# Attention of a decoder trunk: scores, softmax and transposes of two heads together, products with the values by fours

## The chip, the core and the metric

The kernel runs on one core of one Trainium2 chip. The metric is the time of one execution on the device, in microseconds (us). Three runs of the kernel before gave 1165.54, 1167.07 and 1168.0 us; the median is 1167.07.

## What is computed

A trunk of two layers over 256 tokens of width 1024, in float32. Each layer is a half-step SwiGLU feed-forward, a mixer, and another half-step feed-forward, each behind an adaptive RMS norm. The mixer of layer 0 is a gated MLP, that of layer 1 is the attention that the change is about. It has 16 heads of 64, one key block of 256 keys, so that each query sees the causal part of its own block, with a bias by head and distance:

```
q, k, v = split(h @ w_qkv)                    # 16 heads of 64
logits  = q @ k.T / 8 + rel_bias[bucket(distance)]
logits  = where(distance >= 0, logits, -1e30)
o       = softmax(logits) @ v
x       = x + gate * (o @ w_o)
```

## The kernel before

All activations lie on chip; the weights stream from memory. Tokens are two tiles of 128 (t = 0, 1). A product (`gemm`) goes over K tiles of 128: `split_weights` loads two K tiles at a time, ScalarE takes the first part of each weight (a cast) and VectorE the second (a subtraction), and TensorE multiplies in three terms (high with both weight parts, low with the first), each instruction 128 x 512. `gemm` is a generator: it yields after each K tile, and `interleave(steps, calls)` puts other work behind a given step in program order. `tick` hangs one piece of background work (the modulation vectors of later sublayers: a load, and two VectorE steps at L114) behind certain K tiles. The program is then scheduled ahead of time: instructions stand in each engine's queue by the order of the program, by when their inputs were expected, and by when buffers come free, so an engine's queue is not the program's order word for word. At run time each queue is worked in order.

The attention is `moba`, from L642. Its stages:

- The product "qk0" gives q and k of heads 0 to 7, "qk1" those of heads 8 to 15, "vv" gives v. `leave_qk` copies q and k out of the accumulators (L654 on VectorE, L656 on ScalarE) into `half_tile` buffers, of which there are four in all. `turn_qk` transposes them (L386) into qT and kT, in which two heads lie one above the other: an even head in partitions 0 to 63, the odd one in 64 to 127.
- `scores(hd)` does one head. For each of the two query blocks: a product of 64 rows, 128 x 128 or 128 x 256 (L676), a reduction on VectorE that adds the bias and gives the negated maximum (L678), the exponential with its sum on ScalarE (L681). Both query blocks lie in the same accumulator bank. Then the reciprocal (L683) and the scaling (L686). Its `lg` is a `half_tile`.
- `turn(hd)` transposes the head's three 128 x 128 blocks of probabilities (L693) and ScalarE copies them out (L702).
- `mix(hd)` multiplies by the values (L712, L713): the output of an even head goes to partitions 0 to 63, that of an odd head to 64 to 127. Behind each fourth head ScalarE copies the bank to oT (L715).
- `project` multiplies oT by w_o, adds the residual and starts the next norm.

There are six accumulator banks ("acc"), of which a product holds four, and two banks for transposes ("tr"). Weights in two parts, the bias of eight heads, and v share eight buffers ("hl"). Step n of qk1 carries the scores of one head and the transposes of the head two before, and so does each step of vv, some with two. The first fifteen heads' transposes thus run beside products; the products with the values come after vv, in the first two steps of `project` too. The second half of the bias is loaded behind step 5 of qk1.

Of the kernel before, what the change touches and what calls it, by code (L numbers as in the profile page):

```python
# [40 lines left out]
def bucket_onehot():  # L41
    """Column i stands for the distance i - 127; the columns of negative distances are zero."""
    m = np.zeros((NBUCK, EW), np.float32)
    for n in range(S):
        if n < MAX_EXACT:
            b = n
        else:
            b = MAX_EXACT + int(
                math.log(n / MAX_EXACT) / math.log(MAX_DIST / MAX_EXACT) * (NBUCK - MAX_EXACT)
            )  # L50
        m[min(b, NBUCK - 1), P - 1 + n] = 1.0
    return m
# [3 lines left out]
def trunk(ctx: ExitStack, tc: tile.TileContext, x, c, rel_bias, mod_w, mod_b, norm_g,  # L56
# [18 lines left out]
    def small(name, w=1):  # L75
        return stat.tile([P, w], F32, tag=f"st{w}", name=name)
# [16 lines left out]

# [1 line left out]
    def mod_unit(i, s, part):  # L95
        """Steps that end with vector `part` of sublayer (i, s) over all partitions."""
        col = (s * 3 + part) * D
# [51 lines left out]

# [1 line left out]
    raws = {}  # L151
    ready = {}

    def split_weights(src, key, kt, cols):
        """K tile kt of the columns in cols, [P, 2 parts, columns]; a load carries two K tiles."""
        if (key, kt) in ready:
            return ready.pop((key, kt))
        w = sum(cw for _, cw in cols)
        if kt % 2 == 0:
            if w > 512:  # L160
                r = pool.tile([P, 2, D], F32, tag="raw", name=f"raw_{key}_{kt}", bufs=3)
            else:
                r = pool.tile([P, 2, 512], F32, tag="ahl", name=f"raw_{key}_{kt}", bufs=4)
            n = min(2, src.shape[0] // P - kt)
            runs, o = [], 0
            for c0, cw in cols:
                if runs and runs[-1][0] + runs[-1][1] == c0:
                    runs[-1][1] += cw
                else:
                    runs.append([c0, cw, o])  # L170
                o += cw
            for c0, cw, o in runs:
                nc.sync.dma_start(
                    r[:, :n, o:o + cw],
                    src[kt * P:(kt + n) * P, c0:c0 + cw].rearrange("(k p) n -> p k n", p=P))
            raws[key] = r
        r = raws[key]
        hl = hl_slot([P, 2, D], F32R, f"hl_{key}_{kt}")
        nc.scalar.copy(hl[:, 0, :w], r[:, kt % 2, :w])  # L179
        nc.vector.tensor_sub(hl[:, 1, :w], r[:, kt % 2, :w], hl[:, 0, :w].bitcast(F32))  # L180
        return hl
# [5 lines left out]
    def gemm(src, key, cols, lhs, ps, lead_first=0, lead_last=0, early=0, after_first=None, ticks=4):  # L187
        """Fills ps with accumulators [P tokens, columns] by (token tile, column range)."""
        nk = src.shape[0] // P
# [68 lines left out]
    def row_rstd(t, name):  # L258
        """(mean of squares + eps) ** -0.5 of a row of x"""
        ss = []  # L260
# [15 lines left out]
    def to_columns(src, hi, lo, name):  # L276
        """[P tokens, 4 * P] -> two exact parts of its transpose."""
        ps = tr_bank(f"tr_{name}")
# [55 lines left out]
    def act_lhs(a):  # L334
        """Two exact parts of stored activations, by pairs of K tiles."""
        pairs = {}
# [20 lines left out]
    def project(i, s, src, a, lead=LEAD, early=0):  # L357
        """Steps of the product that ends a sublayer, its residual and the next adaLN."""
        ps = {}
# [12 lines left out]
    def interleave(steps, calls):  # L372
        """calls[n] come after step n."""
        for n, _ in enumerate(steps):
            for f, *a in calls.get(n, ()):
                f(*a)
# [4 lines left out]
    def store_act(a, src, w, k0, t, name):  # L381
        """[P tokens, w] -> a[:, k0.., tokens of t]"""
        n = w // P
# [8 lines left out]

# [1 line left out]
    def ffn_gate(g, n, w):  # L394
# [32 lines left out]
    def head(w_in):  # L427
        """The first adaLN by blocks of columns, its products running as the blocks come."""
        src = mod_w[0].rearrange("(p k) n -> p k n", k=KD)
# [105 lines left out]

# [1 line left out]
    def gmlp(i, s):  # L537
# [78 lines left out]

# [1 line left out]
    bias = {}  # L618

    def bias_table():  # L620
        """Scaled bias by head and distance, in DRAM; what the mask hides is at the start."""
        oh = half_tile("oh")[:NBUCK, :EW]
# [12 lines left out]
    def load_bias(b):  # L635
        """[query, head, distances that go down with the key]"""
        bias[b] = hl_slot([P, HEADS // 2, S], F32, f"bias{b}")
# [4 lines left out]
    def moba(i, s):  # L642
# [7 lines left out]
        def leave_qk(n, t, ps):  # L650
            for h in range(2):
                rows[n, t, h] = half_tile(f"q{n}{t}{h}")
                if h == 0:
# [11 lines left out]

        def scores(hd):
            j, po = hd // 2, (hd % 2) * HD
            ps = acc_bank(f"sc{hd}")
            lg = half_tile(f"lg{hd}")
            nm, z, rz = (small(f"{a}{hd}", 2) for a in ("nm", "z", "rz"))  # L670
            b = bias[hd // 8][:, hd % 8, :]
            for qb in range(NT):
                n = P * (qb + 1)
                sl = slice(off[qb], off[qb] + n)
                one = slice(qb, qb + 1)
                nc.tensor.matmul(ps[:, sl], qT[po:po + HD, j, qb * P:(qb + 1) * P],  # L676
                                 kT[po:po + HD, j, :n], start=True, stop=True)
                nc.vector.tensor_tensor_reduce(  # L678
                    lg[:, sl], ps[:, sl], b[:, n - 1::-1], scale=-(HD ** -0.5), scalar=-NEG,
                    op0=ALU.add, op1=ALU.min, accum_out=nm[:, one])  # L680
                nc.scalar.activation(lg[:, sl], lg[:, sl], AF.Exp, bias=nm[:, one], scale=-1.0,  # L681
                                     accum_out=z[:, one])
            nc.vector.reciprocal(rz, z)  # L683
            for qb in range(NT):
                sl = slice(off[qb], off[qb] + P * (qb + 1))
                nc.vector.tensor_scalar_mul(lg[:, sl], lg[:, sl], rz[:, qb:qb + 1])  # L686
            probs[hd] = lg

        def turn(hd):
            pr = probs.pop(hd)  # L690
            tp = tr_bank(f"tp{hd}")
# [12 lines left out]

        def mix(hd):
            j, po = hd // 2, (hd % 2) * HD
            if hd % 4 == 0:
                ovs[0] = acc_bank(f"ov{hd}")
            o = ovs[0][po:po + HD, (j % 2) * S:(j % 2) * S + S]
            pT, vs = pTs.pop(hd), held["v"]  # L710
            cols = slice(hd * HD, (hd + 1) * HD)
            nc.tensor.matmul(o, vs[:, 0, cols], pT[:, 0:S], start=True, stop=False)  # L712
            nc.tensor.matmul(o[:, P:], vs[:, 1, cols], pT[:, S:S + P], start=False, stop=True)  # L713
            if hd % 4 == 3:
                nc.scalar.copy(oT[:, j - 1:j + 1, :], ovs[0].rearrange("p (j n) -> p j n", j=2))  # L715

# [6 lines left out]
                        ticks=2, after_first=lambda: leave_qk(1, 0, qk2)), {  # L723
            0: [(turn_qk, 0, 0), (turn_qk, 0, 1), (scores, 0)], 1: [(scores, 1)],
            2: [(scores, 2), (turn, 0)], 3: [(scores, 3), (turn, 1)],
            4: [(scores, 4), (turn, 2)], 5: [(scores, 5), (turn, 3), (load_bias, 1)],
            6: [(scores, 6), (turn, 4)]})
        leave_qk(1, 1, qk2)
        vp = {}

        def leave_v(t):
            if t == 0:
# [5 lines left out]
                        after_first=lambda: leave_v(0)), {  # L738
            0: [(scores, 7), (turn, 5), (turn_qk, 1, 0), (turn_qk, 1, 1)],
            1: [(scores, 8), (turn, 6), (scores, 9)], 2: [(scores, 10), (turn, 7)],  # L740
            3: [(scores, 11), (turn, 8)], 4: [(scores, 12), (turn, 9)],
            5: [(scores, 13), (turn, 10), (scores, 14), (turn, 11)],
            6: [(scores, 15), (turn, 12)]})
        leave_v(1)
        turn(13)
        for hd in range(5):
            mix(hd)
        turn(14)
        for hd in range(5, 8):
            mix(hd)  # L750
        turn(15)
        interleave(project(i, s, w_o, oT, early=4),
                   {0: [(mix, 8), (mix, 9), (mix, 10), (mix, 11)],
                    1: [(mix, 12), (mix, 13), (mix, 14), (mix, 15)]})

# [1 line left out]
    new_hT()  # L757
# [43 lines left out]
```

## Time and profile before

| | before |
|---|---|
| runs (three), us | 1165.54, 1167.07, 1168.0 |
| median, us | 1167.07 |
| the profiled execution, span from the first to the last instruction, us | 1163.7 |
| the profiled execution, time of its own | not given beside the span |
| TensorE busy | 1139.9 us, 98% |
| TensorE weight loads | 946.8 us, 81% |
| VectorE busy | 828.7 us, 71% |
| ScalarE busy | 592.8 us, 51% |
| GpSimd busy | 32.2 us, 3% |
| mean DMA rate | 241 GB/s |

Times in the profile count from the start of the span. TensorE's matmuls are pipelined: their records overlap, so the time between the starts of two neighbours tells more than the length of one. A float32 matmul stands as two records. "idle before" an instruction is the time its engine stood still, with what released it.

### The profile page before, as it was taken

The page shows a single profiled execution, that of the slowest core. Times are in us where ns is not written, and L with a number is a line of the kernel's source. Part 1 is how long each engine was busy: PE and PEld are TensorE (multiplying, and loading weights), DVE is VectorE, ACT ScalarE, POOL GpSimd, SP SyncE. Part 2 cuts the span into 40 slices and gives each one's busy share as a digit, 9 for nine tenths or more (in the row PEclk, how much of TensorE's full clock was granted, in tenths as well). Part 3 has the DMA queues.
Part 4 walks back from the last instruction along what each step waited for, and adds up shares of the span by engine and source line. Part 5 has one row for each costly group of instructions (what it writes and reads, how often), then busy time and mean ns, then how long its engine had stood idle before and what let it go on. Part 6 is the DMA issues. An engine that isn't in the chain of part 4 may idle for free.

```text
span 1163.7 us, 14007 instructions
## 1 busy us (share of the span) xinstructions
PE 1139.9 (98%) x5381; PEld 946.8 (81%) x5381; DVE 828.7 (71%) x1008; ACT 592.8 (51%) x849; POOL 32.2 (3%) x42
## 2 busy tenths in 40 slices
PE   6999999999999999999999999999999999999997
PEld 4788998878878887888988788998777678889985
DVE  3887787935797888584778776678888668554553
ACT  3465454446555544563553545555366466554541
POOL 0000000000000000000000000000000000000000
PEclk9999999999999999999999999999999999999999
DMA  9787888548688585784978657687696355555640
GB/s 336 274 347 266 302 317 305 198 152 276 225 329 325 215 327 201 269 286 139 316 254 325 219 195 260 205 299 281 229 331 222 131 181 169 176 176 166 217 145 37
DMA packets 86538, 279.99 MB, mean 241 GB/s; under 512 B 4980, under 2 KB 15284, under 8 KB 86472
## 3 DMA queue, kind: packets, MB, share of 16 engines
q1 hardware_dynamic: 86472, 279.10, 68.4%
q8 instruction: 42, 0.69, 0.2%
q14 instruction: 24, 0.20, 0.0%
HBM read 278.01 MB, written 1.07 MB: 240 GB/s over the span
## 4 chain that ended last, share of the span: by engine, by line
PE 90%; DVE 5%; DMA 2%; issue 1%; POOL 1%; ACT 1%; SPq 0%; POOLq 0%; DVEq 0%
PE ps_o L201 24%; PE ps_g L201 19%; PE ps_u L201 19%; PE ps_gu L201 6%; PE ps_v L201 5%; PE ps_qk L201 3%; PE ps_vv L201 2%; PE ta L386 2%; DMA mw<-in_mod_w_dram 2%; PE sc L676 1%; PE mps L132 1%; DVE hl_g L180 1%; PE hps L465 1%; PE sv L609 1%; PE ps_u00a L201 1%
## 5 line engine op out<-in xcount | busy, mean ns | idle before, releaser
L201 PE MATMUL ps_o<-hl_o,ahl 128*128 128x512 f32 x1440 | 334.4, 391 | 0.9 <-ACT ahl L342 0.9
L201 PEld LDWEIGHTS ps_o<-hl_o,ahl 128*128 128x128 f32 x1440 | 269.0, 188 | 56.2 <-ACT ahl L342 1.1
L201 PE MATMUL ps_g<-hl_g,hTh 128*128 128x512 f32 (+1 forms) x768 | 203.7, 376 | 0.7 <-ACT hTh L498 0.7
L179 ACT CAST hl_o<-raw_o 128x1024 fp32r<-128x1024 f32 x120 | 125.9, 1053 | 112.7 <-PE ps_o L201 72.4
L180 DVE TENSOR_TENSOR hl_o<-raw_o,hl_o 128x1024 fp32r<-128x1024 f32 x120 | 145.9, 1222 | 50.2 <-ACT hl_o L179 49.5
L201 PE MATMUL ps_u<-hl_u,hTh 128*128 128x512 f32 (+1 forms) x704 | 181.5, 369 | 0.0
L114 DVE SCALAR_TENSOR_TENSOR ma<-mw,cs,ma 128x1024 f32<-128x1024 f32 x128 | 163.9, 1280 | 15.9 <-DMA mw<-in_mod_w_dram 15.4
L201 PEld LDWEIGHTS ps_g<-hl_g,hTh 128*128 128x128 f32 x768 | 141.6, 189 | 21.7 <-ACT hTh L498 1.4
L180 DVE TENSOR_TENSOR hl_g<-raw_g,hl_g 128x1024 fp32r<-128x1024 f32 (+1 forms) x96 | 107.6, 1132 | 56.7 <-ACT hl_g L179 56.3
L201 PEld LDWEIGHTS ps_u<-hl_u,hTh 128*128 128x128 f32 x704 | 129.7, 188 | 17.6
L179 ACT CAST hl_g<-raw_g 128x1024 fp32r<-128x1024 f32 (+1 forms) x96 | 91.9, 980 | 101.7 <-PE ps_u L201 88.2
L180 DVE TENSOR_TENSOR hl_u<-raw_u,hl_u 128x1024 fp32r<-128x1024 f32 (+1 forms) x88 | 98.5, 1127 | 61.5 <-ACT hl_u L179 60.8
L201 PE MATMUL ps_g<-hl_g,hTl 128*128 128x512 f32 (+1 forms) x384 | 121.3, 376 | 0.0
L179 ACT CAST hl_u<-raw_u 128x1024 fp32r<-128x1024 f32 (+1 forms) x88 | 85.5, 974 | 61.5 <-PE ps_g L201 56.2
L201 PE MATMUL ps_u<-hl_u,hTl 128*128 128x512 f32 (+1 forms) x352 | 108.6, 369 | 0.0
L201 PEld LDWEIGHTS ps_g<-hl_g,hTl 128*128 128x128 f32 x384 | 71.3, 189 | 11.1 <-issue 1.3
L201 PEld LDWEIGHTS ps_u<-hl_u,hTl 128*128 128x128 f32 x352 | 65.4, 188 | 8.7
L201 PE MATMUL ps_gu<-hl_gu,hTh 128*128 128x512 f32 x192 | 55.0, 394 | 0.0
L201 PE MATMUL ps_v<-hl_v,hTh 128*128 128x512 f32 x192 | 54.2, 392 | 0.3 <-ACT hl_v L179 0.3
L180 DVE TENSOR_TENSOR hl_v<-raw_v,hl_v 128x1024 fp32r<-128x1024 f32 x24 | 28.8, 1221 | 27.4 <-ACT hl_v L179 25.0
L201 PEld LDWEIGHTS ps_v<-hl_v,hTh 128*128 128x128 f32 x192 | 35.8, 188 | 8.2 <-ACT hl_v L179 0.5
L201 PEld LDWEIGHTS ps_gu<-hl_gu,hTh 128*128 128x128 f32 x192 | 35.8, 188 | 7.1
(160 smaller groups left out, 1226.3 us busy)
## 6 DMA issues: line engine op xcount, KB each, us to landing
mw<-in_mod_w_dram SPq DMA_DIRECT2D x64, 1024.0 KB
raw_o<-in_ffn_w_out_dram SPq DMA_DIRECT2D x44, 1024.0 KB
raw_g<-in_ffn_w_in_dram SPq DMA_DIRECT2D x32, 1024.0 KB
raw_u<-in_ffn_w_in_dram SPq DMA_DIRECT2D x28, 1024.0 KB
raw_g<-in_ffn_w_in_dram SPq DMA_DIRECT2D x16, 768.0 KB
raw_u<-in_ffn_w_in_dram SPq DMA_DIRECT2D x16, 768.0 KB
raw_v<-in_gmlp_w_in_dram SPq DMA_DIRECT2D x12, 1024.0 KB
raw_gu<-in_gmlp_w_in_dram SPq DMA_DIRECT2D x12, 1024.0 KB
```

Source lines behind the costliest of these rows:

```text
L114: nc.vector.scalar_tensor_tensor(st["acc"], w[:, j, :], cs[:, k0 + j:k0 + j + 1], st["acc"], op0=ALU.mult, op1=ALU.add)
L132: nc.tensor.matmul(ps, lhs, hl[:, j, sl], start=j == 0, stop=j == 1)
L179: nc.scalar.copy(hl[:, 0, :w], r[:, kt % 2, :w])
L180: nc.vector.tensor_sub(hl[:, 1, :w], r[:, kt % 2, :w], hl[:, 0, :w].bitcast(F32))
L201: nc.tensor.matmul(ps[t, h][:, :cw], lhs(k, t)[p], hls[k][:, wp, o:o + cw], start=k == 0 and p == 0 and wp == 0, stop=k == nk - 1 and p == 1)
L386: nc.tensor.transpose(ps[:, j * P:(j + 1) * P], src[:, j * P:(j + 1) * P], ident)
L465: nc.tensor.matmul(ps[part], cb[:, k, :], w[:, k, :], start=False, stop=k == KD - 1)
L609: nc.tensor.matmul(sv[:, sl], wsT[:, g, :], v[n][:, t, lo - n * D:hi - n * D], start=True, stop=True)
L676: nc.tensor.matmul(ps[:, sl], qT[po:po + HD, j, qb * P:(qb + 1) * P], kT[po:po + HD, j, :n], start=True, stop=True)
```

## The change

`scores` takes a pair of heads: all four products of the pair come first, alternating between the two heads, each head in a bank of its own; the reductions and exponentials of both heads follow. The reciprocal and the scaling become a function of their own, `norm`, one step later. `turns` transposes both heads of a pair, two steps behind its scores. `mix` takes four heads at a time. The rows of q and k go to the buffers "sg" (four, used by the gates of the feed-forward and by the last transposed probabilities) and no longer to the four `half_tile` buffers. The second half of the bias is loaded behind step 3 of qk1, before behind step 5. The diff also drops comments and docstrings all through the file, which moves line numbers.

```diff
-                rows[n, t, h] = half_tile(f"q{n}{t}{h}")
+                rows[n, t, h] = pool.tile([P, 512], F32, tag="sg", name=f"q{n}{t}{h}", bufs=4)
...
-        def scores(hd):
-            j, po = hd // 2, (hd % 2) * HD
-            ps = acc_bank(f"sc{hd}")
...
-                nc.tensor.matmul(ps[:, sl], qT[po:po + HD, j, qb * P:(qb + 1) * P],
-                                 kT[po:po + HD, j, :n], start=True, stop=True)
...
+        def scores(pair):
+
+            hds = (2 * pair, 2 * pair + 1)
+            ps, lg = {}, {}
+            for hd in hds:
+                ps[hd] = acc_bank(f"sc{hd}")
             for qb in range(NT):
                 n = P * (qb + 1)
                 sl = slice(off[qb], off[qb] + n)
...
+                for hd in hds:
+                    po = (hd % 2) * HD
+                    nc.tensor.matmul(ps[hd][:, sl], qT[po:po + HD, pair, qb * P:(qb + 1) * P],
+                                     kT[po:po + HD, pair, :n], start=True, stop=True)
...
+            for hd in hds:
+                lg = half_tile(f"lg{hd}")
+                nm, z, rz = (small(f"{a}{hd}", 2) for a in ("nm", "z", "rz"))
+                b = bias[hd // 8][:, hd % 8, :]
+                for qb in range(NT):
...
+                    nc.vector.tensor_tensor_reduce(
+                        lg[:, sl], ps[hd][:, sl], b[:, n - 1::-1], scale=-(HD ** -0.5),
+                        scalar=-NEG, op0=ALU.add, op1=ALU.min, accum_out=nm[:, one])
+                    nc.scalar.activation(lg[:, sl], lg[:, sl], AF.Exp, bias=nm[:, one],
+                                         scale=-1.0, accum_out=z[:, one])
+                probs[hd] = (lg, z, rz)
+
+        def norm(pair):
+            for hd in (2 * pair, 2 * pair + 1):
+                lg, z, rz = probs[hd]
+                nc.vector.reciprocal(rz, z)
+                for qb in range(NT):
+                    sl = slice(off[qb], off[qb] + P * (qb + 1))
+                    nc.vector.tensor_scalar_mul(lg[:, sl], lg[:, sl], rz[:, qb:qb + 1])
...
+        def turns(pair):
+            turn(2 * pair)
+            turn(2 * pair + 1)
+
+        def mix(four):
+
+            ov = acc_bank(f"ov{four}")
+            vs = held["v"]
+            for pair in (2 * four, 2 * four + 1):
+                for hd in (2 * pair, 2 * pair + 1):
...
-            0: [(turn_qk, 0, 0), (turn_qk, 0, 1), (scores, 0)], 1: [(scores, 1)],
-            2: [(scores, 2), (turn, 0)], 3: [(scores, 3), (turn, 1)],
-            4: [(scores, 4), (turn, 2)], 5: [(scores, 5), (turn, 3), (load_bias, 1)],
-            6: [(scores, 6), (turn, 4)]})
+            0: [(turn_qk, 0, 0), (turn_qk, 0, 1), (scores, 0)], 1: [(norm, 0)],
+            2: [(turns, 0), (scores, 1)], 3: [(norm, 1), (load_bias, 1)],
+            4: [(turns, 1), (scores, 2)], 5: [(norm, 2)],
+            6: [(turns, 2), (scores, 3)]})
...
-            0: [(scores, 7), (turn, 5), (turn_qk, 1, 0), (turn_qk, 1, 1)],
-            1: [(scores, 8), (turn, 6), (scores, 9)], 2: [(scores, 10), (turn, 7)],
-            3: [(scores, 11), (turn, 8)], 4: [(scores, 12), (turn, 9)],
-            5: [(scores, 13), (turn, 10), (scores, 14), (turn, 11)],
-            6: [(scores, 15), (turn, 12)]})
+            0: [(norm, 3), (turn_qk, 1, 0), (turn_qk, 1, 1)], 1: [(turns, 3), (scores, 4)],
+            2: [(norm, 4)], 3: [(turns, 4), (scores, 5)], 4: [(norm, 5)],
+            5: [(turns, 5), (scores, 6)], 6: [(norm, 6), (scores, 7)]})
         leave_v(1)
-        turn(13)
-        for hd in range(5):
-            mix(hd)
-        turn(14)
-        for hd in range(5, 8):
-            mix(hd)
-        turn(15)
-        interleave(project(i, s, w_o, oT, early=4),
-                   {0: [(mix, 8), (mix, 9), (mix, 10), (mix, 11)],
-                    1: [(mix, 12), (mix, 13), (mix, 14), (mix, 15)]})
+        mix(0)
+        turns(6)
+        mix(1)
+        norm(7)
+        mix(2)
+        interleave(project(i, s, w_o, oT, early=4), {0: [(turns, 7)], 1: [(mix, 3)]})
```

## Rows read from the trace of the kernel before

**Rows 1.** The page: the span, and the shares of the chain that ended last.

```profile
span 1163.7 us, 14007 instructions
PE 90%; DVE 5%; DMA 2%; issue 1%; POOL 1%; ACT 1%; SPq 0%; POOLq 0%; DVEq 0%
```

**Rows 2.** Busy time by stretch: the columns stand in the first line.

```profile
core 0: us, PE busy (x) PEld busy (x) DVE busy (x) ACT busy (x) POOL busy (x), PEclk, DMA share, GB/s
844.00:862.00 18.00, 17.99 (x82) 14.75 (x81) 17.00 (x17) 11.15 (x14) 0.96 (x1) 1.00 0.89 319
...
862.00:934.00 72.00, 71.98 (x315) 48.46 (x313) 51.12 (x134) 42.38 (x101) 0.00 (x0) 1.00 0.56 195
...
934.00:951.00 17.00, 16.07 (x108) 11.52 (x108) 12.51 (x21) 12.66 (x23) 0.00 (x0) 1.00 0.74 241
```

**Rows 3.** The chain in order of time: start, length, what; an undisturbed product.

```profile
1037.70 21.77 PE ps_u L201 x96
```

**Rows 4.** TensorE's timeline, one turn: start, length, line, operation, shape, count.

```profile
877.54 0.49 PE L676 MATMUL sc<-actm 64*128 64x128 f32 x2
877.96 0.55 PE L693 MATMUL tp<-ident,lg 128*128 128x128 f32 x3
878.26 1.17 PE L201 MATMUL ps_qk<-hl_qk,hTh 128*128 128x512 f32 x4
879.27 0.39 PE L201 MATMUL ps_qk<-hl_qk,hTl 128*128 128x512 f32 x1
879.59 0.70 PE L676 MATMUL sc<-actm 64*128 64x256 f32 x2
880.21 0.50 PE L201 MATMUL ps_qk<-hl_qk,hTl 128*128 128x512 f32 x1
880.55 1.09 PE L201 MATMUL ps_qk<-hl_qk,hTh 128*128 128x512 f32 x4
881.48 0.62 PE L201 MATMUL ps_qk<-hl_qk,hTl 128*128 128x512 f32 x2
882.02 0.49 PE L676 MATMUL sc<-actm 64*128 64x128 f32 x2
```

**Rows 5.** Weight loads of scores: by shape (busy, mean ns), then one on the timeline.

```profile
L676 PEld LDWEIGHTS sc<-actm 64*128 64x128 f32 x64 | 9.4, 184 | 10.6 <-issue 6.6 <-DVE lg L686 2.4 <-DVE vs L735 0.4
...
882.02 0.29 PEld L676 LDWEIGHTS sc<-actm 64*128 64x128 f32 x2 [0.36 <-issue]
```

**Rows 6.** TensorE's timeline, products with the values and the gap between them.

```profile
935.20 0.65 PE L712 MATMUL ov<-pT,vs 128*64 128x256 f32 x2
...
936.40 0.32 PE L713 MATMUL ov<-pT,vs 128*64 128x128 f32 x1
936.41 0.43 PE L712 MATMUL ov<-pT,vs 128*64 128x256 f32 x1
...
941.25 0.50 PE L201 MATMUL ps_o<-hl_o,ahl 128*128 128x512 f32 x1 [0.93 <-ACT ahl L342]
...
944.40 0.66 PE L712 MATMUL ov<-actm,vs 128*64 128x256 f32 x4
...
945.91 3.02 PE L201 MATMUL ps_o<-hl_o,ahl 128*128 128x512 f32 x12
```

**Rows 7.** Busy time from 862 to 934 us: tile lg, then L678, L683, L686, L180, L114.

```profile
862.00:934.00 72.00, 6.51 (x36) 3.79 (x36) 17.51 (x58) 16.43 (x60) 1.00 0.56 195
...
862.00:934.00 72.00, 10.86 (x60) 1.00 0.56 195
...
862.00:934.00 72.00, 2.41 (x15) 1.00 0.56 195
...
862.00:934.00 72.00, 7.65 (x28) 1.00 0.56 195
...
862.00:934.00 72.00, 14.39 (x13) 1.00 0.56 195
...
862.00:934.00 72.00, 15.35 (x12) 1.00 0.56 195
```

**Rows 8.** SP's queue: the issue of the bias load of heads 8 to 15.

```profile
861.77 0.37 SPq L639 DMA_DIRECT2D bias<-ed  x1
```

More of the change, by code (lines that the diff above doesn't have):

```diff
@@ L664, in moba @@
         held = {}
-        def scores(hd):
-            j, po = hd // 2, (hd % 2) * HD
-            ps = acc_bank(f"sc{hd}")
-            lg = half_tile(f"lg{hd}")
-            nm, z, rz = (small(f"{a}{hd}", 2) for a in ("nm", "z", "rz"))
-            b = bias[hd // 8][:, hd % 8, :]
+        def scores(pair):
[3 more added lines that the diff above has]
+                ps[hd] = acc_bank(f"sc{hd}")
             for qb in range(NT):
@@ L674, in scores @@
                 sl = slice(off[qb], off[qb] + n)
-                one = slice(qb, qb + 1)
-                nc.tensor.matmul(ps[:, sl], qT[po:po + HD, j, qb * P:(qb + 1) * P],
-                                 kT[po:po + HD, j, :n], start=True, stop=True)
[L678 to L687, printed above, removed]
+                for hd in hds:
+                    po = (hd % 2) * HD
+                    nc.tensor.matmul(ps[hd][:, sl], qT[po:po + HD, pair, qb * P:(qb + 1) * P],
+                                     kT[po:po + HD, pair, :n], start=True, stop=True)
@@ new lines, in scores @@
+            for hd in hds:
[3 more added lines that the diff above has]
+                for qb in range(NT):
+                    n = P * (qb + 1)
+                    sl = slice(off[qb], off[qb] + n)
+                    one = slice(qb, qb + 1)
+                    nc.vector.tensor_tensor_reduce(
[4 more added lines that the diff above has]
+                probs[hd] = (lg, z, rz)
@@ L689, in turn @@
+        def norm(pair):
[5 more added lines that the diff above has]
+                    nc.vector.tensor_scalar_mul(lg[:, sl], lg[:, sl], rz[:, qb:qb + 1])
         def turn(hd):
-            pr = probs.pop(hd)
+            pr = probs.pop(hd)[0]
             tp = tr_bank(f"tp{hd}")
@@ L703, in turn @@
             pTs[hd] = pT
[L705 to L715, printed above, removed]
+        def turns(pair):
[6 more added lines that the diff above has]
+                for hd in (2 * pair, 2 * pair + 1):
+                    po = (hd % 2) * HD
+                    o = ov[po:po + HD, (pair % 2) * S:(pair % 2) * S + S]
+                    pT = pTs.pop(hd)
+                    cols = slice(hd * HD, (hd + 1) * HD)
+                    nc.tensor.matmul(o, vs[:, 0, cols], pT[:, 0:S], start=True, stop=False)
+                    nc.tensor.matmul(o[:, P:], vs[:, 1, cols], pT[:, S:S + P], start=False,
+                                     stop=True)
+            nc.scalar.copy(oT[:, 2 * four:2 * four + 2, :], ov.rearrange("p (j n) -> p j n", j=2))
         qk = {}
```

## The prediction

> **What bounds the kernel now.** I read the chain of work that ended last first. It belongs to TensorE for 90% of the span [rows 1], so a change of the attention stage pays only by what it takes off TensorE's own line there. Then the busy time of each engine by stretch: over the two products that the scores run beside (862 to 934 us) TensorE is busy for 71.98 of 72.00 us, VectorE for 51.12 (71%), ScalarE for 42.38, at a granted clock of 1.00 (the level of 2.4 GHz) in every stretch [rows 2]. Nobody keeps TensorE waiting; what it spends beyond the plain products is the price of the small matmuls between them. The chain gives the price of a plain product, 21.77 us for 96, so 0.227 us [rows 3].
>
> Then TensorE's timeline for one turn of the present pattern, one head's two scores, another head's three transposes and twelve plain products [rows 4]. From one 64x128 score to the next are 4.48 us. Twelve products are 2.72; the transposes take 0.30 (877.96 to 878.26); left are **1.46 us for the two scores of a head**. Each score stands as two instructions. From the start of the 64x128 score to the next operation are 0.42 us, of the 64x256 one 0.62: 0.20 more for two instructions that are 128 columns wider, so a pass costs 0.10 us per 128 columns. A head's pure passes are then 2 x 0.10 + 2 x 0.20 = 0.60; the other 0.86 are fixed costs, 0.43 for each of the two places where TensorE goes over to 64 rows and back. Part of that shows in the weight loads: one takes 184 ns, two take 0.29 us together, so they follow at 0.106 us, and that of a lone score is not hidden [rows 5].
>
> Last the products with the values, where the trace already has two heads together: the two halves of the output's partitions are two column halves of the array, and an instruction of one head starts 10 ns after one of another (936.40, 936.41). Four heads take 944.40 to 945.91, 1.51 us [rows 6]. They have the same pass lengths as scores, 4 x 0.60 = 2.40 one after another, 1.20 two by two: so 1.20 plus 0.31 fixed. Overlap of two heads in half arrays is real in this kernel, for columns.
>
> **The change, part by part.** Nothing is added or taken out: 32 scores, 48 transposes, 32 products with the values, all reductions, exponentials and copies remain, each of its old size. Order and buffers change.
>
> *Scores.* Before, the second score of a head writes the bank that VectorE has just to read, so it stands apart; 16 heads make 32 places. After, the four scores of a pair are issued before either bank is read, and alternate between partitions 0 to 63 and 64 to 127, two banks. That makes 8 places. No row of before shows two row halves overlapping, so the price of a pair (now 2 x 1.46 = 2.92 us) is bounded. Best: passes overlap and loads hide, as for the values: 0.60 + 0.31 = 0.91, which saves 8 x 2.01 = 16.1 us. Worst: no overlap, every load bare: 1.20 + 8 x 0.106 + 0.23 (the 0.43 less its own two loads) = 2.28, which saves 5.1. I take overlapping passes paced by loads: eight loads at 0.106 are 0.85, longer than the 0.60 of the passes, plus a last pass of 0.20 and the 0.23: 1.28 us, **-13.1 us**. I choose it because overlap is in the trace [rows 6], and so is a load pace [rows 5] that a 128-column load has and a 64-column load of the values need not have.
>
> The Trainium skill, page "TensorE: Matmul & The Clock Gate", section "Part 3: Packing small matmuls — row/col tiling", says that matmuls in different row groups run together at a few ns each beyond the first. By that rule the pair costs about the best end, and the sum below would be -13.8 instead of -10.8 (an estimate). The trace agrees for column halves [rows 6]; no run here shows row halves yet.
>
> *Transposes.* Six together instead of three, at 0.10 each as now. Now they share a changeover with a score [rows 4]; where the order of two heads' transposes and four scores leaves them alone, they pay one of their own: between 0 and 8 x 0.23 = 1.8. I take +0.8.
>
> *Values.* Before, head 0 goes alone at 935.20 [rows 6], and eight heads are spread over three pieces. After there are four pieces of four. One fixed 0.31 less and a lone head that finds a partner (0.30): **-0.6**. Ends: 0 and -1.2.
>
> *End of the stage.* The one idle gap before the output product, 0.93 us at 941.25 [rows 6], waits for ScalarE's first part of the activations. After, two more fours and six transposes (over 3 us) stand between the copy of the first four and that product: **-0.9**. Late next would be the last pair, which cannot be turned before its norm; 24 products of the value projection and three fours lie between, and cover it. Without that cover it would be a wait of one pair's chain, 3.6 us (below).
>
> *Rows of q and k in another buffer.* Same copies, same durations; they no longer queue for the four buffers of the probabilities, and the other buffer's last users, the gates of the feed-forward, are long done. 0; plain products hide the copies now and later.
>
> *Second bias load*, two steps earlier in the program. Its issue on SP's queue stands at 861.77 [rows 8], ahead of the first score: what places it is a free buffer and not the step, and the weight loads behind it on SP keep their order. 0. If it did hold a weight buffer longer, the cover is the three loads ahead. POOL has nothing in this stage that moves.
>
> *New waits.* A pair's norm now stands one step after its scores, and its transposes two steps: 24 products, 5.44 us, where a head had two turns, 8.96 [rows 4]. VectorE's work stays, so its share rises to 51.1 of about 60 us, 85%. Lower end: 844 to 862 us, VectorE busy for 17.00 of 18.00 and TensorE still for 17.99 [rows 2], so 0. Upper end: the first rival. I am nearer to the lower row: 0.26 us for each of 8 pairs, plus 0.43 at each of the two seams where a product's four banks change owners and a pair may not get both of its banks at once: **+3.0**.
>
> Sum: -13.1 + 0.8 - 0.6 - 0.9 + 3.0 = **-10.8 us** on the profiled execution's span of 1163.7, so 1152.9. The page gives no total for that execution; the median of the runs, 1167.07, is 3.4 above the span, which I keep as what lies around it: **1156.3 us**.
>
> **Rivals.**
> *VectorE and ScalarE become the bound of each pair (slower).* Place: TensorE at the first transpose of a pair. A pair's chain is one head's reductions, 10.86/15 = 0.72 us; two heads' exponentials, 2 x 16.43/15 = 2.19; one head's norm, 2.41/15 + 7.65/14 = 0.71: 3.62 us, inside 5.44. But both queues run in order, and in two steps VectorE also has two weight parts at 14.39/13 = 1.11 and two modulation steps at 15.35/12 = 1.28, together 4.78 [rows 7]. The reductions and the norm's reciprocal wait in that queue for TensorE and ScalarE, and a weight part queued behind a waiting reciprocal is late for the next product. If all four long ones come between the links, the chain is 8.40, TensorE waits 2.96 at each of 8 pairs, 23.7 us against 13.8 gained: +9.9, **1177.0 us**. It decides from 13.8/8 = 1.73 us of waiting per pair, three of the four. Against it: TensorE's busy time has no hole today [rows 2]. Chance 0.15.
> The Trainium skill, page "TensorEngine Tiling (Array Packing)", section "Performance Considerations", warns of this: tiling speeds up TensorE and not the emptying of its banks, which may become the bottleneck. The trace so far speaks the other way, with 29% of VectorE free [rows 2].
>
> *Pairs stand together but do not overlap.* The change then gives only fewer changeovers: 1.20 + 0.43 = 1.63 per pair, -10.3 in place of -13.1, so -8.0: **1159.1 us**. For it: no row of row halves. Chance 0.16.
>
> *It does not do what it says:* no overlap, and loads as bare as those of lone scores. -5.1 in place of -13.1, so -2.8: **1164.3 us**. For it: the second load of a 64-row score does not hide today [rows 5]. Chance 0.12.
>
> *Loads hide as well:* the best end, -13.8: **1153.3 us**. Chance 0.10.
>
> **How the numbers follow.** My forecast has 0.47. 0.2% (2.3 us) is about what a measurement of this kernel can tell from no change. Faster by more: 0.47 + 0.10 + 0.16 + 0.05 of the third rival = 0.78. Within: 0.07 of the third and 0.03 of the first (waits that just cancel) = 0.10. Slower: 0.12. The range goes from 1152.0 (the best end with a little less waiting) to 1166.0 (the third rival with a little more); beyond lie the first rival and a small rest, under 0.2.
>
> **What would show it.** Right: over the same two products, pairs of score instructions in different partitions starting some 10 to 100 ns apart, blocks of eight that last about 1.3 us to the next operation, eight such blocks; the stage that now runs from 862 to 951 us some 11 us shorter; TensorE's row still without holes; no gap ahead of the output product. Wrong: blocks of 1.6 or 2.3 us (no overlap, bare loads); scores that stand in twos with products between (the two banks do not come together); idle TensorE ahead of transposes, released by VectorE (the first rival), or ahead of products, released by a late weight part. The forecast falls if the stages outside 862 to 951 us change by more than a microsecond, since nothing here touches them.

## The result, and the profile after

| | before | after |
|---|---|---|
| runs, us | 1165.54 to 1168.0 (4) | 1154.01 to 1154.63 (4) |
| median, us | 1166.53 | 1154.14 |
| ratio to before | | 0.9897, 95% interval [0.9885, 0.9908] |
| span of the profiled execution, us | 1163.7 | 1152.6 |
| TensorE busy, us | 1139.9 | 1127.5 |
| VectorE busy, us | 828.7 | 827.9 |

The change makes the kernel 12.4 us faster; forecast were 10.8 us (1156.3, range 1152 to 1166). The page of after, its span and the shares of its chain, beside [rows 1]:

```profile
span 1152.6 us, 14008 instructions
PE 86%; DVE 7%; DMA 3%; ACT 2%; issue 1%; POOL 1%; SPq 0%; POOLq 0%; DVEq 0%
```

I compare the stage itself, from the first transpose of q to the end of the last product with the values: 861.58 to 950.35 us before, 863.06 to 939.22 after, so 88.77 and 76.16 us, **12.6 us less**. Behind it both kernels take 213.4 us. Ahead of it the execution profiled after is 1.5 us later, and so already at the first long product (73.05 against 71.44 us), where both do the same; start times of the stage lie between 860.2 and 864.4 us in the profiles below. So I go by lengths of the stage and not by spans. The prediction had named a change of more than a microsecond outside the stage as a sign against it; behind the stage there is none, and ahead of it the 1.5 us lie within that spread of 4.2 us.

TensorE's timeline of after, one turn of two heads, answers to [rows 4]:

```profile
900.24 0.82 PE L706 MATMUL tp<-ident,lg 128*128 128x128 f32 x6
900.98 0.93 PE L677 MATMUL sc<-actm 64*128 64x128 f32 x8
901.84 1.20 PE L201 MATMUL ps_vv<-hl_vv,hTh 128*128 128x512 f32 x4
...
907.42 0.81 PE L706 MATMUL tp<-ident,lg 128*128 128x128 f32 x6
908.17 0.93 PE L677 MATMUL sc<-actm 64*128 64x128 f32 x8
909.03 1.20 PE L201 MATMUL ps_vv<-hl_vv,hTh 128*128 128x512 f32 x4
```

From 900.24 to 907.42 are 7.18 us. 24 plain products are 5.44 of them, six transposes 0.60 at their old price; 1.14 are left for the four scores of a pair, where two heads paid 2.92. The block of eight score records lasts 0.86 us from its start to the next operation; six pairs stand so. Pairs 0 and 1 are torn: pair 0, still on TensorE's timeline, comes in two, because its 256-column half needs keys that ScalarE is still copying (why pair 1 is torn I did not find):

```profile
866.11 0.49 PE L677 MATMUL sc<-actm 64*128 64x128 f32 x4
866.53 0.73 PE L201 MATMUL ps_qk<-hl_qk,hTl 128*128 128x512 f32 x2
867.19 0.70 PE L677 MATMUL sc<-actm 64*128 64x256 f32 x4
867.82 1.20 PE L201 MATMUL ps_qk<-hl_qk,hTh 128*128 128x512 f32 x4
```

The busy times of the engines while the two products run (columns as in [rows 2]), first up to the end of the value product, then over the whole stage after and, last, before:

```profile
862.00:923.00 61.00, 60.77 (x320) 46.98 (x320) 50.56 (x129) 39.84 (x98) 0.00 (x0) 1.00 0.67 241
863.06:939.22 76.16, 73.70 (x422) 56.88 (x420) 62.91 (x155) 53.25 (x122) 0.00 (x0) 1.00 0.66 232
...
861.58:950.35 88.77, 87.82 (x421) 59.84 (x419) 63.40 (x154) 54.51 (x121) 0.00 (x0) 1.00 0.59 204
```

VectorE's share went from 71 to 83% (50.56 of 61.00), TensorE's row stays full. But for 0.17 us at the transposes of q and k, only the end has holes. TensorE's timeline there, in answer to [rows 6]:

```profile
922.82 0.93 PE L677 MATMUL sc<-actm 64*128 64x128 f32 x8
923.67 0.66 PE L732 MATMUL ov<-pT,vs 128*64 128x256 f32 x4
...
925.17 0.87 PE L706 MATMUL tp<-ident,lg 128*128 128x128 f32 x6
...
929.87 0.61 PE L706 MATMUL tp<-ident,lg 128*128 128x128 f32 x3 [1.02 <-ACT actm L715]
931.69 3.02 PE L201 MATMUL ps_o<-hl_o,ahl 128*128 128x512 f32 x12 [1.21 <-ACT ahl L342]
```

Two waits for ScalarE, 2.23 us, stand where one of 0.93 stood before. ScalarE's queue in those microseconds shows what stood ahead of the copies:

```profile
923.28 3.90 ACT L179 CAST hl_o<-raw_o 128x1024 fp32r<-128x1024 f32 x4
927.08 0.40 ACT L690 ACTIVATE lg<-lg,nm 128x128 f32<-128x128 f32 x1
...
927.96 0.57 ACT L735 COPY actm<-ov 128x512 f32<-128x512 f32 x1
...
929.32 0.46 ACT L715 COPY actm<-tp 128x384 f32<-128x384 f32 x1
929.67 0.48 ACT L715 COPY pT<-tp 128x384 f32<-128x384 f32 x1
930.05 1.07 ACT L735 COPY actm<-ov 128x512 f32<-128x512 f32 x2
931.00 0.63 ACT L342 CAST ahl<-actm 128x512 fp32r<-128x512 f32 x1
```

The first four's output was complete at 925.17 and is copied at 927.96; the transposes of pair 6, issued from 925.17 on, are copied at 929.32. Ahead of both stand four casts of output weights and exponentials of pair 7. And ScalarE came to them late. VectorE began the reductions of pair 6 only 2.05 us after that pair's scores had started on TensorE (916.29), because two modulation steps, which had waited for their load, stood ahead of them:

```profile
915.82 2.61 DVE L114 SCALAR_TENSOR_TENSOR ma<-mw,cs,ma 128x1024 f32<-128x1024 f32 x2 [0.76 <-DMA mw<-in_mod_w_dram]
918.34 0.28 DVE L687 CUSTOM_DVE_ANT_0 lg<-sc,bias 128x128 f32<-128x128 f32 x1
```

What that was worth shows in the run with the rows' buffer undone, below.

### The profile page after: what moved, and what is told of

Read it like the earlier page. It is cut to its first block, busy times and chain, and to the rows that moved or that the text cites. A ratio compares the mean times of both kernels' runs of the same rounds, so it can differ in the third digit from the quotient of the medians.

```text
span 1152.6 us, 14008 instructions
## 1 busy us (share of the span) xinstructions
PE 1127.5 (98%) x5381; PEld 944.6 (82%) x5381; DVE 827.9 (72%) x1008; ACT 591.3 (51%) x849; POOL 32.2 (3%) x42
## 3 DMA queue, kind: packets, MB, share of 16 engines
HBM read 278.01 MB, written 1.07 MB: 242 GB/s over the span
## 4 chain that ended last, share of the span: by engine, by line
PE 86%; DVE 7%; DMA 3%; ACT 2%; issue 1%; POOL 1%; SPq 0%; POOLq 0%; DVEq 0%; ACTq 0%
PE ps_o L201 27%; PE ps_g L201 19%; PE ps_u L201 19%; PE ps_v L201 5%; PE ps_gu L201 4%; PE ps_qk L201 3%; DMA mw<-in_mod_w_dram 2%; PE ta L386 2%; PE mps L132 1%; PE hps L465 1%; DVE ma L114 1%; DVE hl_g L180 1%; PE ps_u00a L201 1%; PE ps_u00b L201 1%; PE sv L609 1%
## 5 line engine op out<-in xcount | busy, mean ns | idle before, releaser
L180 DVE TENSOR_TENSOR hl_o<-raw_o,hl_o 128x1024 fp32r<-128x1024 f32 x120 | 146.0, 1223 | 52.5 <-ACT hl_o L179 51.7
L114 DVE SCALAR_TENSOR_TENSOR ma<-mw,cs,ma 128x1024 f32<-128x1024 f32 x128 | 163.9, 1280 | 13.0 <-DMA mw<-in_mod_w_dram 12.3
L180 DVE TENSOR_TENSOR hl_g<-raw_g,hl_g 128x1024 fp32r<-128x1024 f32 (+1 forms) x96 | 107.7, 1133 | 57.9 <-ACT hl_g L179 57.6
L180 DVE TENSOR_TENSOR hl_u<-raw_u,hl_u 128x1024 fp32r<-128x1024 f32 (+1 forms) x88 | 98.5, 1127 | 61.9 <-ACT hl_u L179 61.0
L180 DVE TENSOR_TENSOR hl_v<-raw_v,hl_v 128x1024 fp32r<-128x1024 f32 x24 | 28.9, 1222 | 27.3 <-ACT hl_v L179 27.3
```

Source lines behind the costliest of these rows:

```text
L114: nc.vector.scalar_tensor_tensor(st["acc"], w[:, j, :], cs[:, k0 + j:k0 + j + 1], st["acc"], op0=ALU.mult, op1=ALU.add)
```

## The experiments

The theory that went into them was that of the prediction: fewer changeovers, and two row halves that work at once. Rivals: the gain is all changeovers; the gain is all overlap; the buffers bring it; VectorE's chain already decides.

### Both heads of a pair in the same half

```diff
+        def heads(pair):
+            a = 4 * (pair // 2) + pair % 2
+            return a, a + 2
...
-            hds = (2 * pair, 2 * pair + 1)
+            hds = heads(pair)
...
```

> The changed kernel with pairs of heads (0,2), (1,3), (4,6) and so on, so that both heads of a pair lie in the same 64 partitions; order, banks and counts otherwise as after the change. Overlap theory (the two row halves of the array work at once, that is most of the gain): a block of eight score instructions grows from 0.86 us to between 1.6 (loads hidden) and 2.3 us (loads bare), over 8 pairs 6 to 11 us more than the changed kernel, so about 1160 to 1165 us, ratio to before 0.995 to 0.999. Changeover theory (the gain is that TensorE goes over to 64 rows 8 times and not 32 times): block at most 1.0 us, time within 1.5 us of the changed kernel, ratio about 0.990.

1155.85 us, ratio 0.9906 [0.9893, 0.9920]; stage 78.82 us. TensorE's timeline of this run, one turn:

```profile
900.52 0.82 PE L710 MATMUL tp<-ident,lg 128*128 128x128 f32 x6
901.27 1.57 PE L681 MATMUL sc<-actm 64*128 64x128 f32 x8
902.77 1.20 PE L201 MATMUL ps_vv<-hl_vv,hTh 128*128 128x512 f32 x4
...
908.37 0.82 PE L710 MATMUL tp<-ident,lg 128*128 128x128 f32 x6
```

The block grows from 0.86 to 1.50 us and the turn from 7.18 to 7.85, so overlap is real and worth 0.67 us per whole pair, 5.4 us for eight. In the stage, idle time left out, it is 4.3 us, the torn pairs having less to lose. The stage is only 2.7 us longer than after, since just 0.7 of the 2.4 us that TensorE idled there are left here. Neither theory had that. The two medians differ by 1.7 us, but the intervals of the two ratios overlap, so the loss is read from the timeline and not from the total. As the main source of the gain, overlap falls; as a part of it, it is shown.

### One head at a time, its two scores in two banks

Made on the kernel before.

```diff
-            ps = acc_bank(f"sc{hd}")
+            pss = [acc_bank(f"sc{hd}{qb}") for qb in range(NT)]
...
```

> The kernel before, one head at a time, with one edit: the two query blocks of a head in two banks in place of one, so that its two scores can stand together. No pairs, so nothing in different row halves. Changeover theory: 14 of 16 heads pay one changeover in place of two, at the 0.43 us read from the kernel before (0.64 with the load that stays bare behind it in the pair runs): 6 to 9 us faster than the kernel before, ratio 0.992 to 0.995, block of a head's two scores 0.8 to 0.9 us. Rival (the separate place cost little, the gain is all from overlap of two heads): within 1.5 us of the kernel before.

1162.06 us, ratio 0.9964 [0.9952, 0.9975]; stage 84.28 us, 4.5 less than before. One turn of this run, the twelve products left out:

```profile
877.65 0.92 PE L674 MATMUL sc<-actm 64*128 64x128 f32 x4
878.50 0.55 PE L696 MATMUL tp<-ident,lg 128*128 128x128 f32 x3
878.80 1.18 PE L201 MATMUL ps_qk<-hl_qk,hTh 128*128 128x512 f32 x4
...
881.74 0.92 PE L674 MATMUL sc<-actm 64*128 64x128 f32 x4
```

4.09 us where [rows 4] have 4.48: 0.39 us per head, 6.2 for sixteen; the stage got less since some heads stayed torn and 1.09 us of idle time came up at the end. The miss is in the total, some 4 us where 6 to 9 were expected; the size per place (0.43 expected, 0.39 measured) holds. And the block of one head's scores lasts 0.85 us, that of a pair's after the change 0.86: the second head rides free.

### Head by head within a pair

```diff
-            for qb in range(NT):
...
-                for hd in hds:
+            for hd in hds:
+                po = (hd % 2) * HD
+                for qb in range(NT):
...
```

> The changed kernel with the four scores of a pair issued head by head (both query blocks of the first head, then both of the second) in place of alternating heads. Overlap theory with instructions started in order: only the two middle scores can overlap, the passes of a pair take 1.0 (0.2 + 0.4 + 0.4) in place of 0.6 us, and two loads in a row of one half stay bare: a block of 1.2 to 1.5 us, 3 to 5 us more than the changed kernel, 1157 to 1159 us. If TensorE sorts the halves by itself: block 0.86 us, no difference (below 1 us). Changeover theory: no difference.

1153.09 us, ratio 0.9880 [0.9863, 0.9896]; stage 74.61 us. In TensorE's queue of this run, from pair 2 on, both scores of the first head precede both of the second; that is read from the program as it is scheduled, since the trace does not tell the heads apart. Its timeline, the whole block and then two narrow looks at starts inside one:

```profile
899.48 0.93 PE L677 MATMUL sc<-actm 64*128 64x128 f32 x8
900.34 1.20 PE L201 MATMUL ps_vv<-hl_vv,hTh 128*128 128x512 f32 x4
...
880.16 0.39 PE L677 MATMUL sc<-actm 64*128 64x128 f32 x2
...
880.48 0.39 PE L677 MATMUL sc<-actm 64*128 64x256 f32 x2
```

Again 0.86 us. At 880.16 two 128-column records start, one of each head (with all four scores in one half, in the run above, neighbours start at least 0.11 us apart), although the first head's 256-column score stands between them in the queue; the two 256-column records start together at 880.48. So what I wrote of the queues, that each is worked in order, does not hold here for TensorE's starts in two different halves. The halves run beside each other in both orders that I tried; what both share is that the two heads stand in the queue together. The theory of starts in order falls.

### The two buffer edits alone, and the rows' buffer undone

The first on the kernel before, the second on the changed one:

```diff
-                rows[n, t, h] = half_tile(f"q{n}{t}{h}")
+                rows[n, t, h] = pool.tile([P, 512], F32, tag="sg", name=f"q{n}{t}{h}", bufs=4)
```

> The kernel before with two parts of the change alone: rows of q and k in the other buffer, second bias load two steps earlier. My theory (both parts cost and bring nothing by themselves): within 1 us of the kernel before, ratio 0.999 to 1.001. Rival (the accumulator banks freed earlier at the seam of the two products are a good part of the gain): 3 us or more faster, ratio 0.997 or lower.

1163.22 us, ratio 0.9972 [0.9961, 0.9982]; stage 86.20 us, 2.6 less than before. **My zero was wrong here**: the idle 0.93 us at the end are gone, and in the order that the queues got with these edits, scores of two heads stand next to each other at two places of TensorE's timeline and overlap. Each block holds a 128-column score of one head and a 256-column score of another:

```profile
910.14 0.70 PE L676 MATMUL sc<-actm 64*128 64x256 f32 x4
...
925.62 0.70 PE L676 MATMUL sc<-actm 64*128 64x128 f32 x4
```

The rival's size came, not its mechanism: of the 2.6 us, 0.9 are the idle time and the rest fits these two places; nothing here shows that banks came free earlier.

> The changed kernel with the rows of q and k back in the four buffers that the probabilities use. My theory (the other buffer brings nothing, TensorE's queue keeps its order and the copies have time): within 1 us of the changed kernel, ratio to before 0.989 to 0.991. Rival (pairs hold all four buffers, so the rows wait for the transposes of a pair, hold the accumulators, and TensorE waits at the seam): 2 to 5 us slower than the changed kernel, with idle TensorE ahead of the first products of the value projection or of the transposes of q and k.

1152.00 us, ratio 0.9874 [0.9859, 0.9889]; stage 74.81 us. With pairs the old buffer costs nothing. So the two edits together are a gain for the order before (which of them brings it was not separated), and the rows' buffer is none for the order after; the parts don't add.

The stage is even 1.35 us shorter than after, more than my theory allowed, and the buffer is not the reason. The instructions stand in the same order as after in the queues of TensorE, VectorE and ScalarE from pair 6's scores to the output product, the copies on ScalarE too. But the reductions of pair 6 began 1.11 us behind the start of its scores, where after took 2.05, and the wait ahead of the transposes is 0.07 us in place of 1.02. TensorE's and VectorE's timelines of this run:

```profile
914.43 0.93 PE L677 MATMUL sc<-actm 64*128 64x128 f32 x8
...
915.54 0.28 DVE L687 CUSTOM_DVE_ANT_0 lg<-sc,bias 128x128 f32<-128x128 f32 x1
...
927.06 0.61 PE L706 MATMUL tp<-ident,lg 128*128 128x128 f32 x3
928.88 3.04 PE L201 MATMUL ps_o<-hl_o,ahl 128*128 128x512 f32 x12 [1.21 <-ACT ahl L342]
```

So, by these two profiles, about one microsecond of after's 2.23 goes back to when VectorE got to pair 6, and the other 1.21 stand in both runs.

### More work on VectorE

```diff
                 nc.vector.reciprocal(rz, z)
+                for _ in range(1):
+                    nc.vector.tensor_scalar_mul(lg[:, :3 * P], lg[:, :3 * P], 1.0)
```

> The changed kernel with one needless multiplication by 1.0 over a head's 128 x 384 probabilities in its norm: some 0.45 us more on VectorE per head, 7 us in all, in the chain from a pair's scores to its transposes. Slack theory (the chain fits inside the two steps with room, VectorE has free time): at most 2 us more than the changed kernel, 1154 to 1156 us, no TensorE idle released by VectorE before the last two pairs. Bound theory (the chain already ends last at each pair): 5 to 7 us more, 1159 to 1161 us.

1153.91 us, ratio 0.9891 [0.9876, 0.9905]; stage 75.30 us: no loss, as the slack theory had it.

> The same with two needless multiplications, 14 us more on VectorE, so that its work in the stage (62.9 + 14 us) comes to the stage's length of 76 us. Slack theory: this is past the point where it decides, 4 to 10 us more than the changed kernel, with idle TensorE ahead of transposes or products. Bound theory: twice the cost of one, 10 to 14 us more.

1152.37 us, ratio 0.9878 [0.9864, 0.9893]; stage 74.45 us. Busy times of this run by stretch: first all engines, then VectorE in the added line alone:

```profile
862.00:923.00 61.00, 60.69 (x323) 46.66 (x323) 54.82 (x154) 41.81 (x100) 0.00 (x0) 1.00 0.66 235
...
862.00:923.00 61.00, 8.96 (x28) 1.00 0.66 235
```

The added operations are shorter than I put them, 0.32 us (8.96 for 28), so some 10 us in all and not 14. With them VectorE is busy for 90% of the stretch and TensorE loses nothing in it. The bound theory falls. The slack theory's loss did not come either, but the load at which it expected one was not reached. The chain of a pair has room for at least 0.64 us more per head; at what load it would end last was not found. The stage is 1.7 us shorter than after, which is idle time again: 0.35 us at the end.

### Pair 7 earlier, and the end pulled forward

```diff
-            2: [(norm, 4)], 3: [(turns, 4), (scores, 5)], 4: [(norm, 5)],
-            5: [(turns, 5), (scores, 6)], 6: [(norm, 6), (scores, 7)]})
+            2: [(norm, 4)], 3: [(turns, 4), (scores, 5)], 4: [(norm, 5), (scores, 6)],
+            5: [(turns, 5), (norm, 6), (scores, 7)], 6: [(turns, 6)]})
...
-        turns(6)
+        norm(7)
         mix(1)
-        norm(7)
```

> The changed kernel with pair 6 scored one step earlier and pair 7 ahead of the last 24 products of the value projection, as my prediction had wrongly read it; transposes of pair 6 behind the last product. End theory (the idle 2.2 us before the output product come from pair 7's reductions and exponentials, which stand ahead of the copies in the queues of VectorE and ScalarE after the last product): idle time there falls below 0.7 us, 1.5 to 2.5 us faster than the changed kernel, 1151.5 to 1152.7 us. Rival (what ends last there is the casts of the output weights on ScalarE): the idle time stays above 1.5 us and the time within 1 us of the changed kernel.

1151.79 us, ratio 0.9866 [0.9846, 0.9885]; stage 75.29 us. Idle before the output product 0.81 us, but 0.35 came up in the value product. The stage is 0.9 us shorter than after, about half of what was expected. Nor does it show that the edit did this, as runs that changed nothing at the end idle there for 0.35 to 1.21 us.

The next puts `norm(7)` behind the first half of the last products, `turns(7)` ahead of the third four, and leaves only the last four inside the output product.

> As the run with pair 7 early, and also pair 7's norm ahead of the second half of those products, its transposes ahead of the third four, and only the last four inside the output product. End theory: idle below 0.5 us, 2 to 3 us faster than the changed kernel, 1151 to 1152.2 us. Rival: as with pair 7 early alone, no gain over the changed kernel.

1151.76 us, ratio 0.9871 [0.9856, 0.9886]; idle at the end 0.56 us. It is no better than the one before, and again within that spread. Then the same with the old buffer for the rows:

> The version with the end pulled forward, and the rows of q and k back in the four buffers of the probabilities, as each of the two was at or below the changed kernel by itself. If the two add: 1150 to 1151 us. If both only took the same idle time at the end: 1151.5 to 1152.5 us, as either alone.

1150.83 us, ratio 0.9872 [0.9854, 0.9890]; nothing idle at the end. The medians would fit a sum of both; the ratios don't tell the three apart.

### The end's copies on VectorE

```diff
+            if hd < 12:
                 nc.scalar.copy(pT[:, :3 * P], tp[:, :3 * P])
+            else:
+                nc.vector.tensor_copy(pT[:, :3 * P], tp[:, :3 * P])
...
```

The output copy of the first four likewise.

> The changed kernel with three kinds of copies at the end on VectorE in place of ScalarE: the transposed probabilities of heads 12 to 15 and the first four's output. ScalarE theory (the 2.2 us of idle TensorE before the output product are waits for ScalarE's queue, in which four weight casts and a pair's exponentials stand ahead of these copies, while VectorE has room): idle falls below 1 us, stage 74.5 to 75.2 us in place of 76.2, 1152 to 1153 us. Rival (VectorE's own queue, with the reductions and weight parts, is what ends last there): idle unchanged or longer, no gain.

1151.33 us, ratio 0.9875 [0.9857, 0.9893]; stage 74.00 us, 2.2 less than after. TensorE's timeline at the end of this run:

```profile
926.63 0.44 PE L736 MATMUL ov<-actm,vs 128*64 128x128 f32 x4
927.41 3.04 PE L201 MATMUL ps_o<-hl_o,ahl 128*128 128x512 f32 x12 [0.33 <-ACT ahl L342]
```

The wait ahead of the transposes is gone and the other shrinks from 1.21 to 0.33 us. The first part says nothing of the copies, since that wait is gone with the rows' buffer undone too. The second is the effect of the edit as far as it is shown: beside that run, whose reductions of pair 6 come as early as here, the copies moved off ScalarE go with 0.9 us less idle time, so ScalarE's queue ended last there, and VectorE had room for the copies. It rests on one profile of each.

By their medians this version and the one with the end pulled forward and the old buffer are the shortest that I ran, both clear of the kernel before. But the intervals of all the variants of the changed kernel touch or overlap that of the changed kernel ([0.9885, 0.9908]), and the runs of a single one, the latter, spread over 4.1 us (1149.36 to 1153.46). So a gain over the changed kernel is not shown; what differs in the profiles of the variants that keep the pairs and the last products in place is the idle time, while TensorE's busy time in the stage stays within half a microsecond of 73.7.

## Why the prediction was right

**What bounds it.** TensorE's line in the stage, and what is taken off it shows in the time: it holds. In the stage TensorE's busy time fell by 14.1 us and the stage by 12.6; the 1.5 us between are idle time. That busy time and total both fell by 12.4 us over the whole kernel is a coincidence.

**Scores, forecast -13.1, measured -14.2** (8 pairs at 2.92 - 1.14). The mechanism held; the term was 1.1 us too small. I let the loads of eight records follow one another at 0.106 us and set the pair at 1.28. The loads of the two halves run side by side. TensorE's weight loads show eight in 0.52 us after, and eight in 1.17 with both heads in the same half:

```profile
881.65 0.52 PEld L677 LDWEIGHTS sc<-actm 64*128 64x128 f32 x8 [0.17 <-issue]
...
901.26 1.17 PEld L681 LDWEIGHTS sc<-actm 64*128 64x128 f32 x8 [0.17 <-issue]
```

That goes the way of my fourth rival, at 0.10, but not to its price: 1.14 us lies between its 0.91 and my 1.28. The Trainium skill, page "TensorE: Matmul & The Clock Gate", section "Part 3: Packing small matmuls — row/col tiling", says a second row group costs next to nothing; the trace agrees, 0.86 us for a pair's block beside 0.85 for a single head's. The experiments split the term along the way: from 2.92 us for two heads to 2.14 (twice 1.07: 4.09 less 12 products and three transposes) when each head's two scores stand together, to 1.81 when the pair stands together in one half, to 1.14 with overlap. For eight pairs that is 6.2, 2.6 and 5.4 us. So nearly two thirds of the gain are changeovers, which the reading of [rows 4] had at 0.43 us a place.

**Values, forecast -0.6, measured about -0.9**: three pieces of 1.50, 2.8 and 1.50 us (the middle one two fours) against 6.7 us in five pieces.

**Transposes and new waits, forecast +0.8 and +3.0**: the whole stage gave -12.6; scores, values and the end below come to -13.6, which leaves +1.0 for both. The torn pairs 0 and 1 account for it, as was put for the seams, though not for the reason put there: pair 0 lacks keys and not a bank. The share for VectorE's chain (2.1 us) was not needed between the products. For the pairs that products cover, the first rival falls by the run with two extra operations a head; in the profile of after, the two modulation steps that it named did come between pair 6's scores and its reductions, with the cost at the end told above.

**The end, forecast -0.9, measured +1.5: the step that failed, with the wrong sign** (2.40 us idle in the stage against 0.93; 0.17 of it lies at the transposes of q and k). The prediction said of the last pair that "24 products of the value projection and three fours lie between, and cover it". The three fours do, the 24 products do not. The calls of step 6 come behind the last products of vv, not ahead of them: the loop yields inside its last block only where `early` asks for it. On the timeline pair 7's scores stand at 922.82, right behind the value product. And I looked at the order of TensorE's work there but not at ScalarE's queue, where four casts and pair 7's exponentials stand ahead of the copies. Of the 2.23 us, about 1.0 come from VectorE's late reductions of pair 6 and need not recur; the other 1.2 are ScalarE's queue, and moving the copies to VectorE left 0.33. How much idle time there is at the end changes with small edits elsewhere, by the order that the queues get ahead of time and by when loads land: 0.35 to 1.21 us in runs with pairs that changed nothing there.

**Buffers of the rows and second bias load, forecast 0 each.** Right for the changed order, wrong by themselves: the two alone on the kernel before bring 3 to 4 us. In the sum this hid, since that gain is in part of the same kind as the scores' and is contained in it. The reason given for the bias load was wrong: "what places it is a free buffer and not the step". Its issue stood 0.2 us behind the start of the stage before and stands 3.2 us ahead of it (863.06) after, so the step does place it (with the rows' buffer undone it stands just as early):

```profile
859.85 0.37 SPq L639 DMA_DIRECT2D bias<-ed  x1
```

**From the span to the time, +3.4.** This set the span of one execution against the median of three. The execution profiled after took 1154.63 us for its span of 1152.6, so 2.0; the term was 1.4 us too large.

The forecast came as close as it did partly by luck, because errors offset each other: the scores gave 1.1 us more, the values 0.3 more, and the transposes and waits cost 2.8 less than put, while the end cost 2.4 us more.

## What to carry to other kernels

Small matmuls in half of the array, spread one by one among large ones, cost more by the changes of shape around them than by their own passes (here 0.86 of 1.46 us per head). Read the price of such a place as the difference of two starts, and gather the small matmuls before thinking of overlap. Where two heads lie in different halves, getting both into the queue together was enough here, and the second was then nearly free. When the bound engine gets faster, look next at the in-order queue of each engine that empties its banks at the stage's end, and look up in the loop behind which product a call really comes. Before crediting an edit with a wait that is gone, look whether it is gone in runs without that edit too.

## What the hardware showed that I had not expected

Two row halves don't wait for each other's place in the queue: with the scores issued head by head, the second head's first score started at 880.16 with the first head's, ahead of a score that stood before it, and the block lasted 0.86 us as before. Weight loads of the two halves overlap too, eight in 0.52 us, where eight of one half take 1.17. And VectorE at 90% busy over the two products (862 to 923 us), with its work in the chain of every pair, cost TensorE nothing there.
